# Two layers of a diffusion trunk on one core: the order of transposes, early blocks and residual loads at the seams between stages

## The chip, the cores and the metric

The kernel runs on one core of a Trainium2 chip. The metric is the device time of one execution in microseconds (us); several executions are timed, and the median is given. The engines are called TensorE (PE in the rows), VectorE (DVE), ScalarE (ACT), GpSimd (POOL) and SyncE (SP, which issues most DMAs).

## The reference

Two layers over 1024 latent tokens and 256 context tokens, all of width 1024. The parts that matter here:

```python
for l in range(DEPTH):
    mod = act_lat @ w_mod[l] + b_mod[l]          # shifts, scales and gates of the layer
    sh1, s1, g1, sh2, s2, g2 = [m[:, None, :] for m in jnp.split(mod, 6, axis=-1)]
    ...
    mix = jnp.concatenate([y_pool, y_na, y_gqa], axis=-1) @ w_out[l]
    x = layer_norm(DEEPNORM_ALPHA * x + g1 * mix, ln1_g[l], ln1_b[l])
    ffn = conv_ffn(x * (1 + s2) + sh2, w_up[l], conv_w[l], conv_b[l], w_down[l])
    x = layer_norm(DEEPNORM_ALPHA * x + g2 * ffn, ln2_g[l], ln2_b[l])
```

conv_ffn is an up-projection to 2 x 2816 columns, a convolution of width 3 along the tokens, a * silu(g), and a down-projection. The context tokens go through the same layer with their own modulation, except the last part of layer 1.

## The kernel before, in words

A product in the kernel is exact to float32: each operand is split into a high and a low part (names ending in h and l, `split`: ScalarE makes the high part, VectorE the low one), and three products are added up in PSUM. One such product of 128 x 128 by 128 x 512 is three matmuls. PSUM is used as four tiles of two banks (128 x 1024 f32), handed out in the order of the program and given back when their reader is done.

**Out-projection** (`OutProj`). Eight latent tiles of 128 tokens, then in layer 0 two context tiles. A tile takes 48 matmuls into `oacc`. The first tiles (5 in layer 0, 3 in layer 1) are run with the weight row k outermost, the others one by one. `norm` of a tile: `s` = `oacc` times gate, the input x added, the layer norm (sums on VectorE, Square on ScalarE, the power on GpSimd), `xm` = s * G on GpSimd and + B on VectorE. Its eight transposes (`tps`) are kept in a list `late` and put into PE's order by `follow`, after a tile's products; with `hold` the last call is left out. `NXM` says how many tiles `xm` there are. From tiles 4 to 7, `sums` also forms the sums T1, T2 and T4 of the fast product below and stores them to DRAM (TX2, TX14).

**Up-projection** (`UpLat`) uses a two-by-two scheme of seven products (Strassen's), in 44 half-width blocks. A first part of a block needs only the first four tiles; `early` does it ahead of its place as cover for the last transposes: 24 matmuls into `oe`, ScalarE's copy and VectorE's addition to `ue`. AHEAD is the number of such blocks; all but two are stored to DRAM (UE) and loaded again in `weights`. `end` puts the remaining transposes (T) and early blocks (E) in order by a string of letters. `enter` loads T1, T2 and T4 again, in a pool that opens once the out-projection's has closed.

**Down-projection** (`DownLat`): seven products of 11 units each, a unit being 12 matmuls and a split of loaded pieces (`hw`). A list `later` holds small work to be done at every second unit: loads of the residual tiles `s` from XS, and `residual`, which multiplies them by ln_g and adds ln_b on VectorE.

**Start**: the first shift and scale of all channels (`modps`), as products of 2 x 128 columns; **context FFN's end** (`tail_c`): norm and modulation of the two context tiles for layer 1.

The tile framework sets each engine's order from the program's order, moving work ahead where its operands allow it; `keep_in_program_order` pins an instruction to its place.

## Time and profile before

| | us |
|---|---|
| median of 3 runs | 2997.43 (2996.47 to 3000.92) |
| profiled execution, its own time | 2999.13 |
| span of that execution | 2997.4 |
| TensorE busy | 2784.9 (93%) |
| VectorE busy | 2285.8 (76%) |
| ScalarE busy | 1492.3 (50%) |
| GpSimd busy | 991.3 (33%) |

The span runs from the first to the last instruction; the time has some 1.7 us around it. The busy shares are averages over stages that have different limits, so the rows below go by stretches. The mean granted clock of TensorE over the span is 0.971 of the full 2.4 GHz.

### The profile page before, as it was taken

Reading aid. Unit: us, or ns where it says so; the run is one execution under the profiler, and the core shown is the slowest. Engines: PE = TensorE matmul, PEld = TensorE weight load, DVE = VectorE, ACT = ScalarE, POOL = GpSimd, SP = SyncE. Lnnn points to the kernel's source line nnn. Section 1 sums busy time; section 2 is a strip of 40 time slices with the busy share of each in tenths; the row PEclk is TensorE's granted clock in tenths of the full one; section 3 lists DMA queues with packets and bytes.
Section 4 is the critical chain, followed back from the end, with each engine's and each line's share of the span. In section 5 each row is a group of like instructions: output and inputs, shape, how many; then the busy total and the mean of one; then the engine's idle time right before and its main releaser. Section 6 shows DMA issues by size and latency. Waiting matters only on the chain.

```text
span 2997.4 us, 41914 instructions
## 1 busy us (share of the span) xinstructions
PE 2784.9 (93%) x14715; PEld 2359.7 (79%) x14715; DVE 2285.8 (76%) x3651; ACT 1492.3 (50%) x2328; POOL 991.3 (33%) x773
## 2 busy tenths in 40 slices
PE   8998889988799999899799799999998899999898
PEld 6798778977578887788788679888987688887676
DVE  4985789956688888756887765699957788887667
ACT  4222888824344444434655422598854444444343
POOL 0304354114345554200253440353133444553001
PEclk9999999998899999999899999999999999999999
DMA  7786662164554444865555588452134444445773
GB/s 275 249 269 192 184 169 85 43 219 154 190 168 155 154 152 158 292 211 185 181 177 183 186 269 289 142 171 83 58 121 137 161 158 158 157 159 179 264 222 129
DMA packets 271686, 531.08 MB, mean 177 GB/s; under 512 B 26778, under 2 KB 110834, under 8 KB 270708
## 3 DMA queue, kind: packets, MB, share of 16 engines
q1 hardware_dynamic: 270180, 524.11, 53.9%
q10 hardware_dynamic: 1296, 4.29, 0.4%
q8 instruction: 117, 1.92, 0.3%
q14 instruction: 93, 0.76, 0.1%
HBM read 394.16 MB, written 134.14 MB: 176 GB/s over the span
## 4 chain that ended last, share of the span: by engine, by line
PE 25%; DVE 15%; DMA 10%; issue 4%; ACT 4%; POOL 2%; SPq 1%; POOLq 0%; DVEq 0%; ACTq 0%
PE o L1363 7%; PE dy L1605 4%; PE dx L1605 3%; DVE wl L177 2%; PE pvs L848 2%; PE oacc L1072 2%; PE s L786 2%; DVE wl L172 2%; PE pt L803 1%; DVE s L1329 1%; DMA raw<-in_wup_dram 1%; DMA wm<-in_wmT_dram 1%; DMA VD<-stB 1%; DMA raw<-in_wdown_dram 1%; DVE w L1329 1%
## 5 line engine op out<-in xcount | busy, mean ns | idle before, releaser
L1329 POOL TENSOR_TENSOR cv<-cv 128x512 f32<-128x512 f32 (+1 forms) x110 | 251.5, 2286 | 262.5 <-DVE cv L1499 126.5
L1363 PE MATMUL o<-mxh,wh 128*128 128x512 f32 x640 | 253.5, 397 | 19.3 <-DVE cv L1499 12.7
L177 DVE TENSOR_TENSOR PT<-pt,PT 128x512 fp32r<-128x512 f32 (+2 forms) x396 | 247.8, 644 | 18.4 <-ACT PT L176 16.2
L1363 PE MATMUL o<-mxl,wh 128*128 128x512 f32 x640 | 252.6, 395 | 0.0
L1363 PE MATMUL o<-mxh,wl 128*128 128x512 f32 x640 | 251.6, 394 | 0.0
L786 PE MATMUL s<-K,q 128*128 128x256 f32 (+2 forms) x960 | 236.8, 359 | 14.6 <-DVE m L753 12.8
L176 ACT CAST wh<-raw 128x512 fp32r<-128x512 f32 (+1 forms) x132 | 119.0, 906 | 216.7 <-PE o L1363 141.1
L794 ACT ACTIVATE P<-P,m 128x1280 f32<-128x1280 f32 (+3 forms) x216 | 221.9, 1028 | 9.5 <-DVE m L753 8.0
L177 DVE TENSOR_TENSOR wl<-raw,wh 128x512 fp32r<-128x512 f32 (+1 forms) x132 | 162.8, 1239 | 75.7 <-ACT wh L176 75.1
L176 ACT CAST PT<-pt 128x512 fp32r<-128x512 f32 (+2 forms) x396 | 205.4, 558 | 26.0 <-PE pt L834 10.4
L848 PE MATMUL pvs<-PT,V 128*128 128x256 f32 (+1 forms) x1488 | 209.9, 289 | 5.0 <-DVE PT L177 2.0
L318 PE MATMUL pacc<-wh,mxh 128*128 128x512 f32 (+1 forms) x512 | 191.8, 375 | 15.5 <-DVE rt L284 7.2
L753 DVE CUSTOM_DVE_ANT_0 P<-s,zero,m 128x512 f32<-128x512 f32 (+1 forms) x288 | 189.0, 656 | 20.7 <-PE s L786 1.1
L172 DVE TENSOR_TENSOR wl<-raw,wh 128x1024 fp32r<-128x1024 f32 (+1 forms) x112 | 151.9, 1367 | 62.4 <-ACT wh L170 61.9
L848 PEld LDWEIGHTS pvs<-PT,V 128*128 128x128 f32 x1488 | 186.2, 191 | 12.2 <-ACT mixr L859 4.6
L320 PE MATMUL pacc<-wh,mxl 128*128 128x512 f32 (+1 forms) x512 | 187.5, 367 | 2.2 <-DVE mxl L177 2.2
L319 PE MATMUL pacc<-wl,mxh 128*128 128x512 f32 (+1 forms) x512 | 187.6, 366 | 0.0
L176 ACT CAST wh<-hw 128x1024 fp32r<-128x1024 f32 x98 | 102.7, 1053 | 160.8 <-PE dx L1605 37.5
L177 DVE TENSOR_TENSOR wl<-hw,wh 128x1024 fp32r<-128x1024 f32 x98 | 125.1, 1286 | 75.2 <-ACT wh L176 74.7
L170 ACT CAST wh<-raw 128x1024 fp32r<-128x1024 f32 (+1 forms) x118 | 119.1, 1018 | 93.4 <-POOL raw L168 23.6
L786 PEld LDWEIGHTS s<-K,q 128*128 128x128 f32 x960 | 140.8, 190 | 29.4 <-DVE m L753 23.1
L803 PE MATMUL pt<-ident,P 128*128 128x128 f32 x1032 | 160.1, 273 | 3.5 <-DVE PT L177 2.5
(355 smaller groups left out, 7849.1 us busy)
## 6 DMA issues: line engine op xcount, KB each, us to landing
raw<-in_wup_dram SPq DMA_DIRECT2D x140, 512.0 KB, 4.7
wm<-in_wmT_dram SPq DMA_DIRECT2D x96, 512.0 KB, 4.9
w<-in_wdown_dram SPq DMA_DIRECT2D x44, 512.0 KB, 3.7
hw<-in_wdown_dram SPq DMA_DIRECT2D x66, 256.0 KB, 3.7
q<-QN SPq DMA_DIRECT2D x96, 128.0 KB, 3.1
q<-QG SPq DMA_DIRECT2D x96, 128.0 KB, 2.7
TD0T<-w SPq DMA_DIRECT2D x44, 256.0 KB, 2.2
hw<-HD0S SPq DMA_DIRECT2D x44, 256.0 KB, 3.2
```

The lines of the kernel that those rows point to most:

```text
L172: (sub or nc.vector).tensor_tensor(out=lo[:, :n], in0=raw[:, :n], in1=h[:, :n], op=ALU.subtract)
L176: nc.scalar.copy(h, src)
L177: nc.vector.tensor_tensor(out=lo, in0=src, in1=h, op=ALU.subtract)
L318: nc.tensor.matmul(acc[:, :n], lhsT=xh[:, i, k, :], rhs=wh[:, o:o + n], start=(k == 0), stop=False)
L753: nc.vector.tensor_tensor_reduce(out=dst, in0=src, in1=bias, scale=-1.0, scalar=init, op0=ALU.add, op1=ALU.min, accum_out=m)
L786: nc.tensor.matmul(s[:, :n], lhsT=q[:, part, c0:c0 + P], rhs=K[:, k0:k0 + n], start=(part == 0), stop=(part == 1))
L794: nc.scalar.activation(out=self.P, in_=self.P, func=AF.Exp, bias=self.m, scale=-1.0, accum_out=self.rsum())
L803: nc.tensor.transpose(pt[:, b, :], self.P[:, p0 + b * P:p0 + (b + 1) * P], ident)
L848: nc.tensor.matmul(self.pv[:, c0:c0 + n], lhsT=V[:, vb, :], rhs=x[:, sl, c0:c0 + n], start=(self.c == 0), stop=(self.c == self.tot - 1),)
L1329: eng.tensor_tensor(out=out, in0=a_, in1=b_, op=op)
L1363: nc.tensor.matmul(o, lhsT=lhsT, rhs=rhs, start=fresh and k == 0 and i == 0, stop=k == 3 and i == 2, skip_group_check=not fresh,)
L1605: nc.tensor.matmul(o, lhsT=x[:, tc_], rhs=w[:, r], start=fresh and j == 0 and i == 0, stop=j == NP - 1 and i == 2, skip_group_check=not fresh,
```

## The change

Transposes of the out-projection are taken from `late` by age (AGE = 3 steps, two steps a tile, one after four weight rows, one after eight) instead of by number; layer 0 has three tiles `xm` instead of two; the last latent tile and the context tiles are multiplied on VectorE while ScalarE squares (`gain`: (s + nm) * G with nm the negative mean; `offset`: times the norm's scale, plus B) instead of on GpSimd after the norm. There are 5 and 6 early blocks instead of 4 and 4, kept in halves of 512 columns, the first stored from ScalarE's queue, and all but the last stored and loaded again. T1 and T2 are loaded during the cover, at the letter X, and only T4 in `enter`. In the down-projection the rows g, ln_g, ln_b and the residual tiles are fetched one at a time between units of products 1 and 3, and `residual` is done in products 2 and 4 and pinned. `modps` takes 64 products of 256 columns with 8 loads of 1 MB instead of 128 and 16. The context FFN's end uses `gain` and `offset` too, and the stores to YN go from SyncE instead of ScalarE.

```diff
-NXM = (2, 3)
+NXM = (3, 3)
...
-AHEAD = (4, 4)
+AHEAD = (5, 6)
+AGE = 3
+DORD = ("PE",)
+UEB = (3, 4)
...
-YQ = 1
+YQ = 0
...
+        if early:
+            early(nm)
...
+            if z.lat and t < 7:
+                ln_add(s, xt, op, xt)
+                f = modulate_T(s, G, B, op, "xm", NXM[self.l], self.ps, *dst, ident, False, mul=nc.gpsimd, sink=sink)
+            else:
+                xm = op.tile([P, D], F32, tag="xm", name="xm", bufs=NXM[self.l])
+                nm, rs = ln_add(s, xt, op, xt, False, lambda nm: gain(xm, s, nm, G))
+                offset(xm, xm, rs, B)
+                nb = op.tile([P, 1], F32, tag="lnb", name="lnb", bufs=LNB)
+                nc.vector.tensor_tensor(out=nb, in0=nm, in1=rs, op=ALU.mult)
+                nc.scalar.activation(out=s, in_=s, func=AF.Identity, bias=nb, scale=rs)
+                f = lambda: transpose_T(xm, self.ps, *dst, ident, False, sink)
+            self.late.append((self.step, f))
             if SILU and not self.silu:
                 self.silu = True
                 one = op.tile([P, 1], F32, name="one")
                 nc.scalar.activation(out=one, in_=s[:, 0:1], func=AF.Silu)
-            sink = (lambda pt: self.sums(mx, t - 4, pt)) if z.lat and t >= 4 else None
-            self.late.append(
-                modulate_T(
-                    s, G, B, op, "xm", NXM[self.l], self.ps, mx[0][:, t], mx[1][:, t], ident, False, mul=nc.gpsimd,
-                    sink=sink,
-                )
-            )
...
-        def follow(self, keep=1):
-            while len(self.late) > (keep if len(self.norms) < 2 else 0):
-                self.late.pop(0)()
+        def follow(self):
+
+            self.step += 1
+            if self.late and self.step - self.late[0][0] >= AGE:
+                self.late.pop(0)[1]()
             while self.norms and len(self.late) < NXM[self.l]:
                 self.norm(*self.norms.pop(0))
 
-        def run(self, z, tiles, mx, xin, x1_dst, kmajor=False, hold=False):
+        def run(self, z, tiles, mx, xin, x1_dst, kmajor=False):
             accs = {}
 
             def acc(t):
@@ -1135,31 +1149,33 @@
             if kmajor:
                 for t in tiles:
                     acc(t)
-                for k in range(7):
+                for k in range(8):
                     for t in tiles:
                         self.product(mx, accs[t], t, k)
                     if self.side:
                         self.side()
+                self.norms += [(z, mx, t, accs[t], xin, x1_dst) for t in tiles]
+                self.follow()
+                return
             for t in tiles:
-                if kmajor:
-                    self.product(mx, accs[t], t, 7)
+                acc(t)
+                for k in range(8):
+                    self.product(mx, accs[t], t, k)
+                    if k == 3:
+                        self.follow()
+                self.norms.append((z, mx, t, accs[t], xin, x1_dst))
+                self.follow()
...
+                elif x == "X":
+                    self.take()
...
+        def take(self, proj, xs):
+
+            self.xs = proj.xs = xs
+            for t in proj.stored:
+                y = rawp.tile([P, 1024], F32, tag="raw", name="xt")
+                nc.sync.dma_start(out=y, in_=TX12[t])
+                for i in range(2):
+                    split(xs[i][0][:, t], xs[i][1][:, t], y[:, 512 * i:512 * i + 512].rearrange("p (k j) -> p k j", k=4))
...
-            u = self.uf.tile([P, 1024], F32, tag="ue", name="ue", bufs=2)
-            nc.scalar.copy(u[:, 0:512], o[:, 0:512])
+            u = self.half()
+            nc.scalar.copy(u, o[:, 0:512])
+            if i:
+                nc.scalar.dma_start(out=UE[self.l, f][0], in_=u)
             self.mm(o[:, 512:1024], a_, 512, "B21", True)
-            tt(nc.vector, u[:, 512:1024], o[:, 512:1024], u[:, 0:512], ALU.add)
-            self.blocks[f] = {"early": u, "u1": u[:, 0:512]}
-            if i >= 2:
-                nc.sync.dma_start(out=UE[self.l, f], in_=u)
-                self.blocks[f] = {"early": None}
+            c = self.half()
+            tt(nc.vector, c, o[:, 512:1024], u, ALU.add)
+            if i:
+                nc.sync.dma_start(out=UE[self.l, f][1], in_=c)
+            self.blocks[f] = {"early": None} if i else {"early": c, "u1": u}
+
+        def half(self):
+            return self.uf.tile([P, 512], F32, tag="ue", name="ue", bufs=UEB[self.l])
 
         def cover(self):
             n = AHEAD[self.l]
-            return [lambda i=i: self.early(i) for i in [*range(2, n), 0, 1]]
+            return [lambda i=i: self.early(i) for i in [*range(1, n), 0]]
...
-                if j % 2 and self.later:
+                if (j % 2 or j and p in (1, 3)) and self.later:
...
-            self.later = [lambda t=t: nc.sync.dma_start(out=s[t], in_=x1[t * P:(t + 1) * P, :]) for t in range(4)]
+            pin = tc.keep_in_program_order
+
+            def fetch(t):
+                return lambda: pin(nc.sync.dma_start(out=s[t], in_=x1[t * P:(t + 1) * P, :]))
             self.product(0, X, True, after=lambda t: nc.scalar.copy(u[t], X[t]))
-            self.later = [lambda t=t: residual(s[t]) for t in range(4)]
+            rows = {}
+            self.later = [
+                lambda: rows.update(ln=self.rows()), lambda: rows.update(g2=self.g2())
+            ] + [fetch(t) for t in range(4)]
             Y = self.banks("dy")
             self.product(1, Y, True, after=lambda t, Y=Y: tt(nc.vector, u[t], Y[t], u[t], ALU.add))
...
-            self.later = [lambda t=t: nc.sync.dma_start(out=s[t], in_=x1[t * P:(t + 1) * P, :]) for t in range(4, 8)]
+            self.later += [lambda t=t: residual(rows["ln"], s[t]) for t in range(4)]
             self.product(2, X, False, after=c11)
-            self.later = [lambda t=t: residual(s[t]) for t in range(4, 8)]
+            self.later += [fetch(t) for t in range(4, 8)]
...
+            self.later += [lambda t=t: residual(rows["ln"], s[t]) for t in range(4, 8)]
             self.product(4, X, True, after=c22)
...
-        tt(nc.vector, x, x, rows[0], ALU.mult)
-        tt(nc.vector, x, x, rows[1], ALU.add)
+        for r, op in zip(rows, (ALU.mult, ALU.add)):
+            tc.keep_in_program_order(nc.vector.tensor_tensor(out=x, in0=x, in1=r, op=op))
...
-                for i, t in enumerate(wms):
-                    nc.sync.dma_start(out=t[:, k, :], in_=a["wm0"][8 * (1 - i) + k])
+                t = wms[k // 4][:, k % 4, :]
+                nc.sync.dma_start(out=t, in_=a["wm0"][k])
                 if k % 4 == 0:
                     craw = pp.tile([P, 4, CTX], F32, tag="st", name="craw", bufs=NST)
                     nc.sync.dma_start(out=craw, in_=a["ctxT"][k:k + 4].rearrange("k p t -> p k t"))
                 raw = craw[:, k % 4, :]
                 mp = ps.tile([P, 1024], F32, tag="mm", name="modps")
-                for i, t in enumerate(wms):
-                    for kk in range(8):
-                        nc.tensor.matmul(
-                            mp[0:2, P * i:P * (i + 1)], lhsT=act[:, kk, :], rhs=t[:, k, kk * P:(kk + 1) * P],
-                            start=(kk == 0), stop=(kk == 7),
-                        )
+                for kk in range(8):
+                    nc.tensor.matmul(
+                        mp[0:2, 0:2 * P], lhsT=act[:, kk, :], rhs=t[:, 2 * P * kk:2 * P * (kk + 1)],
+                        start=(kk == 0), stop=(kk == 7),
+                    )
...
-                proj.run(CTXS, range(2), mxc, xin(a["ctx"][0]), XSC, hold=True)
+                proj.run(CTXS, range(2), mxc, xin(a["ctx"][0]), XSC)
                 wxs.close()
                 xss, xsp = right_pool("xs", 1)
-                proj.xs = quarters(xsp)
-                proj.end(up.cover(), "TETEETE")
+                proj.take = lambda: up.take(proj, quarters(xsp))
+                proj.end(up.cover(), "ETEXTEEE")
...
+                xm = fc.tile([P, D], F32, tag="xm", name="xm", bufs=2)
+                junk = fc.tile([P, D], BF16, tag="junk", name="junk")
+                nm, rs = ln_add(s, o, fc, junk, False, lambda nm: gain(xm, s, nm, GB["c"][0]))
+                offset(xm, xm, rs, GB["c"][1])
+                late.append(lambda: transpose_T(xm, ps, xtc[0][:, t], xtc[1][:, t], ident, False))
...
-                proj.end(up.cover(), "ETEETE")
+                proj.end(up.cover(), "EXTEETEEE")
...
+                if not last:
+                    last.extend(row_tile(fd, t_, a[nm][1]) for nm, t_ in (("ln2_g", "l2g"), ("ln2_b", "l2b")))
```

**PE's order at layer 0's passage.** `oacc` are the out-projection's products, `tps` the transposes, `oe` the early blocks, `o` the first block in its place. Before:

```order
L1072 MATMUL oacc<-wh,mxl 128x512 x2
L252 MATMUL tps<-ident,xm 128x128 x16
L1072 MATMUL oacc<-wh,mxh 128x512 x2
...
L252 MATMUL tps<-ident,xm 128x128 x8
L1363 MATMUL oe<-mxh,wh 128x512
...
L1363 MATMUL oe<-mxl,wh 128x512
L1363 MATMUL oe<-mxh,wl 128x512
L1363 MATMUL o_8846<-T2h,wh 128x512
L1363 MATMUL o_8911<-T2h,wh 128x512
L1363 MATMUL o_8846<-T2l,wh 128x512
```

After:

```order
L1078 MATMUL oacc<-wh,mxl 128x512 x2
L258 MATMUL tps<-ident,xm 128x128 x16
L1078 MATMUL oacc<-wh,mxh 128x512 x2
...
L258 MATMUL tps<-ident,xm 128x128 x8
L1377 MATMUL oe<-mxh,wh 128x512
...
L1377 MATMUL oe<-mxl,wh 128x512
L1377 MATMUL oe<-mxh,wl 128x512
L1377 MATMUL o_8823<-T2h,wh 128x512
L1377 MATMUL o_8823<-T2l,wh 128x512
L1377 MATMUL o_8823<-T2h,wl 128x512
```

The first rows are the end of the products with k outermost: 240 ahead of the first transposes before, 288 now. The second piece holds the last transposes, with 24 products of early blocks between them and the first T2 before and 60 now.

**SyncE's order at layer 0's down-projection.** `hw` are weight pieces, g, ln_g, ln_b and s the rows and residual tiles of 512 KB. Before:

```order
L1586 DMA hw<-HD0S_155 128x512
L224 DMA g_11864<-rows0lat_2627 128x1024
L224 DMA ln_g<-in_ln_g_dram 128x1024
L224 DMA ln_b<-in_ln_b_dram 128x1024
L1645 DMA s_11880<-XS_99 128x1024
L1645 DMA s_11881<-XS_99 128x1024
L1645 DMA s_11882<-XS_99 128x1024
L1645 DMA s_11883<-XS_99 128x1024
L1592 DMA hw<-TD0T_166 128x512
L1586 DMA hw<-HD0S_155 128x512
L1592 DMA hw<-TD0T_166 128x512
```

After:

```order
L1601 DMA hw<-HD0S_155 128x512
L228 DMA ln_g<-in_ln_g_dram 128x1024
L228 DMA ln_b<-in_ln_b_dram 128x1024
L1607 DMA hw<-TD0T_166 128x512
L228 DMA g_12108<-rows0lat_2555 128x1024
L1601 DMA hw<-HD0S_155 128x512
L1607 DMA hw<-TD0T_166 128x512
L1663 DMA s_11832<-XS_99 128x1024
L1601 DMA hw<-HD0S_155 128x512
L1607 DMA hw<-TD0T_166 128x512
L1663 DMA s_11833<-XS_99 128x1024
```

Seven loads stood in a row; now ln_g and ln_b are a pair, and each of the others has pieces of a unit around it. The tiles s of the second half follow in product 3.

**VectorE's order at layer 1's down-projection.** `wl` and `mxl` are the splits that products wait for; rows with ln_g and ln_b are the residual. Before:

```order
L177 TENSOR_TENSOR wl<-hw,wh 128x1024 x3
L1329 TENSOR_TENSOR s_26172<-s_26172,ln_g 128x1024
L1329 TENSOR_TENSOR s_26172<-s_26172,ln_b 128x1024
L1329 TENSOR_TENSOR s_26173<-s_26173,ln_g 128x1024
L1329 TENSOR_TENSOR s_26174<-s_26174,ln_g 128x1024
L1329 TENSOR_TENSOR s_26173<-s_26173,ln_b 128x1024
L1329 TENSOR_TENSOR s_26175<-s_26175,ln_g 128x1024
L1329 TENSOR_TENSOR s_26174<-s_26174,ln_b 128x1024
L177 TENSOR_TENSOR mxl<-hw,mxh 128x1024
L1329 TENSOR_TENSOR s_26175<-s_26175,ln_b 128x1024
```

After:

```order
L181 TENSOR_TENSOR wl<-hw,wh 128x1024
L1343 TENSOR_TENSOR u_26148<-dy_26362,u_26148 128x512
L1760 TENSOR_TENSOR s_26154<-s_26154,ln_b 128x1024
L181 TENSOR_TENSOR mxl<-hw,mxh 128x1024
L1760 TENSOR_TENSOR s_26155<-s_26155,ln_g 128x1024
L181 TENSOR_TENSOR mxl<-hw,mxh 128x1024 x2
L1760 TENSOR_TENSOR s_26156<-s_26156,ln_g 128x1024
L1343 TENSOR_TENSOR u_26147<-dy_26361,u_26147 128x512
L1760 TENSOR_TENSOR s_26155<-s_26155,ln_b 128x1024
L1343 TENSOR_TENSOR u_26149<-dy_26362,u_26149 128x512
L181 TENSOR_TENSOR mxl<-hw,mxh 128x1024
```

Before, seven residual operations stand in a row; now they alternate with splits and with the evictions of product 1 (`u`).

## Rows read from the trace of the kernel before

**Rows 1.** Table by stretches (us), core 0; busy time of each engine, TensorE's granted clock

```profile
core 0: us, PE busy (x) PEld busy (x) DVE busy (x) ACT busy (x) POOL busy (x), PEclk, DMA share, GB/s
12.00:39.00 27.00, 27.00 (x245) 20.24 (x243) 11.59 (x37) 6.67 (x12) 0.00 (x0) 1.00 0.96 366
665.00:751.00 86.00, 66.74 (x300) 54.79 (x299) 54.48 (x90) 42.46 (x52) 38.01 (x23) 0.88 0.48 164
751.00:866.00 115.00, 89.00 (x350) 70.27 (x349) 86.60 (x88) 48.28 (x64) 40.73 (x23) 0.87 0.52 178
866.00:1000.00 134.00, 133.69 (x590) 110.21 (x589) 111.03 (x104) 60.49 (x71) 64.74 (x34) 1.00 0.44 148
1250.00:1300.00 50.00, 40.93 (x163) 32.11 (x162) 37.34 (x34) 19.26 (x22) 0.00 (x0) 0.90 0.76 266
2188.00:2283.00 95.00, 92.49 (x425) 76.76 (x424) 44.45 (x64) 39.39 (x47) 35.21 (x29) 0.98 0.40 132
2283.00:2480.00 197.00, 176.01 (x734) 140.74 (x733) 160.78 (x159) 86.12 (x111) 88.96 (x47) 0.95 0.48 159
2777.00:2820.00 43.00, 29.42 (x108) 22.32 (x109) 30.06 (x26) 14.55 (x16) 0.00 (x0) 0.84 0.78 280
```

**Rows 2.** TensorE's waits by releaser, 665 to 866: us in total, times, longest

```profile
PE tps L252 <- DVE xm L263: 19.3, 5, 13.3
PE o L1363 <- ACT T2h L176: 8.8, 1, 8.8
PE oe L1363 <- ACT ue L1422: 5.5, 2, 4.7
PE tps L252 <- DVE lnm L235: 3.7, 1, 3.7
PE o L1363 <- DVE cv L1499: 3.3, 1, 3.3
PE o L1363 <- ACT u L1443: 3.3, 1, 3.3
PE o L1363 <- DVE T2l L177: 1.5, 1, 1.5
```

**Rows 3.** The same view, 2188 to 2480 us (layer 1's passage)

```profile
PE tps L252 <- DVE xm L263: 9.0, 3, 3.6
PE o L1363 <- ACT T2h L176: 6.0, 1, 6.0
PE o L1363 <- DVE cv L1499: 4.2, 2, 3.5
PE oe L1363 <- ACT ue L1422: 2.1, 2, 1.4
PE o L1363 <- ACT u L1443: 1.8, 1, 1.8
...
```

**Rows 4.** TensorE's timeline: start, us, engine, line, operation, tiles, count, idle before

```profile
699.53 1.06 PE L252 MATMUL tps<-ident,xm 128*128 128x128 f32 x8 [1.20 <-DVE xm L263]
```

**Rows 5.** TensorE's waits by releaser, 1250 to 1300 us (down, layer 0)

```profile
PE dy L1605 <- ACT wh L176: 4.9, 1, 4.9
PE dy L1605 <- DVE wl L177: 4.0, 2, 2.6
```

**Rows 6.** The same view, 2777 to 2820 us (down, layer 1)

```profile
PE dy L1605 <- ACT mxh L176: 8.5, 1, 8.5
PE dy L1605 <- DVE mxl L177: 4.5, 2, 2.6
...
```

**Rows 7.** VectorE's timeline at the start of layer 0's down-projection

```profile
...
1252.82 1.23 DVE L1329 TENSOR_TENSOR s<-s,ln_g 128x1024 f32<-128x1024 f32 x1 [5.24 <-DMA s<-XS]
```

**Rows 8.** Timeline at the end of the context FFN, three engines

```profile
1693.25 2.37 ACT L246 ACTIVATE acc<-acc,lnb,lrs 128x1024 f32<-128x1024 f32 x2
...
1696.80 2.35 DVE L263 TENSOR_TENSOR xm<-xm,ln_b 128x1024 f32<-128x1024 f32 x2
...
1698.16 2.15 PE L252 MATMUL tps<-ident,xm 128*128 128x128 f32 x9 [7.57 <-DVE xm L263]
```

128 lines of the change are left out of this document (53 added, 75 removed).

## The prediction

> **What bounds the kernel now.** I read the page first: TensorE is busy 93% of the span, so the kernel is bound by it wherever nothing interrupts it, and the only time to win lies where it waits or runs slowly. The table by stretches shows where that is [rows 1]. From 866 to 1000 us, inside an up-projection, TensorE is busy 133.69 of 134.00 us at a granted clock of 1.00; its 590 products of 512 columns there cost 133.69 / 590 = 0.2266 us each, my price for one at the full clock, 2.4 GHz. Three kinds of stretch look otherwise: the passage from the out-projection to the up-projection in layer 0 (665 to 866 us) and in layer 1 (2188 to 2480), and the start of each down-projection (1250 to 1300 and 2777 to 2820). There TensorE idles, and the clock column falls to 0.84 to 0.95.
>
> What each costs, from [rows 1] and one price more, 1.06 us for the eight transposes of a tile [rows 4]:
> Layer 0 passage: busy 66.74 + 89.00 = 155.7 of 201 us, idle 45.3. Its 650 records are 80 transposes (ten tiles) and 570 products; at the full clock 570 x 0.2266 + 10 x 1.06 = 139.8, so 15.9 us more went to the half clock (1.2 GHz).
> Layer 1, 2283 to 2480: busy 176.0 of 197; 694 products and some 40 transposes are 162.6, so 13.4 us of half clock and 21 idle.
> Down, layer 0: 40.9 of 50 busy, 163 x 0.2266 = 36.9: 4.0 of clock, 9.1 idle. Down, layer 1: 29.4 of 43, 108 x 0.2266 = 24.5: 4.9 of clock, 13.6 idle.
> Together about 125 us: the most that this change could return there.
>
> The waits by releaser name the idle time. In layer 0 [rows 2]: transposes waiting for the normalised tile (xm, 19.3 us, the longest 13.3), T2h 8.8 and T2l 1.5, an early block's eviction (ue) 5.5, lnm 3.7, then 6.6 for u and cv. In layer 1 the same with smaller sizes [rows 3]: xm 9.0, T2h 6.0, cv 4.2, ue 2.1, u 1.8. At the down-projections the weight pieces are late: wh and wl 8.9 us [rows 5], mxh and mxl 13.0 [rows 6]. Why they are late shows on VectorE: it idles 5.24 us for a residual tile (s<-XS) and then works through residual operations that stand in its queue ahead of the splits the products need [rows 7].
>
> **The change part by part.**
> **Transposes by age, layer 0.** The long wait of 13.3 us is for the first normalised tile, whose time is set by the loads and the chain of the norm, not by TensorE; the change doesn't hasten it. It puts a sixth tile's products into it: 48 x 0.2266 = 10.9 us. Were nothing else in the way, 2.4 us of wait would be left. But all four PSUM tiles are then held by products, and the first transposes need a slot that the eviction of the third tile frees, which itself waits for a buffer s; I take 5 us left, so 8.3 saved. The other 6.0 us of xm waits may return between later tiles, since the norm of a pair of tiles is as long as before; I take none saved. Bounds 0 and 14.
> **S-sums loaded during the cover.** T2h and T2l, 10.3 us, are late because their reloads start only when the out-projection's pool has closed: in PE's order before, 24 early products (5.4 us) lie between the last transposes and the first use of T2. Now the reloads are issued ahead of the last transposes, and 60 products (13.6 us) follow those. I take 10 saved; bounds 6 and 10.3.
> **Fifth early block.** 24 products more (5.4 us) are moved into the passage from the stage behind it, so PE's sum doesn't change; as cover they take from ue 5.5 and lnm 3.7 what isn't VectorE's. The last tiles' multiply leaves GpSimd as well. I take 4 of 9.2; bounds 0 and 9.
> Of the 15.9 us of clock, which goes with the waits, I take 6, near their share (22 of 45 us saved would be 8). Layer 0: -8.3 - 10 - 4 - 6 = **-28**, bounds -10 and -50.
> **Layer 1.** T2h -6; of xm's 9.0 us -4 (the transposes are already spread there, the change shifts them by half a tile); ue and u -1; clock -5 of 13.4. **-16**, bounds -6 and -32.
> **Down-projections.** Before, SyncE issues g, ln_g, ln_b and four s tiles, seven of 512 KB, in a row ahead of the next weight pieces. At 366 GB/s, the rate of a stretch with the DMA engines 0.96 busy [rows 1], these 3.67 MB hold the pieces back by 10 us; the wait was 8.9 and 13.0. Now one such tile goes with each unit, and a unit lasts 12 x 0.2266 = 2.72 us: 0.52 MB of it and 0.52 MB of pieces take 2.87 us, 0.15 over for each of some seven units. That is nearly no slack, but the pieces are fetched ahead. The residual operations now lie in product 2 and product 4, one operation between two splits by pinning: 11 splits and 8 residual operations of 1.23 us [rows 7] and 8 half-wide additions (half of it, an estimate) are 28.3 us in 11 x 2.72 = 29.9 us of products. It fits, barely; were it uncovered, it would cost 3 us a layer. Layer 0: 7 of 9.1 idle and 3 of 4.0 clock, **-10** (bounds -4, -13). Layer 1: 10 of 13.6 and 4 of 4.9, **-14** (bounds -6, -18).
> **Context FFN's end.** TensorE waits 7.57 us for xm, behind a ScalarE pass of 2.37 us and two multiplies of the same length that now run beside the squares [rows 8]. Up to 4.7 leave the chain, but VectorE has to find room for the multiply; **-3**, bounds -1 and -4.7.
> **Start.** TensorE is back to back there: 245 records in 27.00 us are 110 ns each [rows 1], or 0.86 ns a column, twice the 0.443 of the 512-column products. So columns set it, and half as many records save next to nothing; the first transfer is 0.52 MB longer, 1.4 us at 366 GB/s. **+1**, bounds -1 and +2.
> **Queues.** The YN stores go from ScalarE's queue to SyncE's, the first halves of the early blocks the other way; weight loads may now stand behind a store that waits for its data. I take 0, bounds -1 and +3.
> Sum: -28 - 16 - 10 - 14 - 3 + 1 = **-70** on the profiled execution's 2999.13 us: 2929. The median, 2997.43, lies 1.7 below it, so I predict **2928**.
>
> **The rivals.**
> *VectorE takes over.* It was busy 86.6 of 115 us and 160.8 of 197 in the passages, and each wait filled leaves it less time. If only T2, half of the down terms and the context's end return: -10 - 6 - 12 - 3 = -31, with some clock **2964**. Against it: 866 to 1000 runs TensorE without waits with VectorE at 111 of 134, 83%; layer 0's 141 us of work in 173 would be 82%.
> *The waits are cut into small ones and the clock stays low.* The clock terms (6 + 5 + 3 + 4 = 18) don't come: -52, **2947**. The row against it is 2188 to 2283, where transposes and products already alternate on the same four PSUM tiles, at 0.98. The Trainium skill, "TensorE: Matmul & The Clock Gate", section "A second HAM failure mode: psum-queue depth-cycling", says that cycling through PSUM can make TensorE pause between groups so often that the gain is lost to re-throttling. By that rule this rival would be the likeliest; the row just named doesn't bear it out.
> *More than I take.* All xm and ue waits vanish with most of the clock: layer 0 -48, layer 1 -28, down -30, the rest -3: -109, **2890**. For it, nothing in TensorE's own work stands against it (its products at the full clock leave 125 us unused); against it, the first tile's norm, which no early block hastens.
> *Slower.* One mechanism: the early blocks kept in DRAM (four and five) are reloaded in halves into three or four buffers on SyncE's queue. If a reload waits there for its buffer, the block's weight loads wait behind it, and TensorE with them. It cancels the gain at 70 / 9 = 8 us a block; at 9 us, **3009**. For it, weights loaded once a block; against it, two or three blocks of 13 us lie between a buffer's use and its reload.
> *No change to speak of.* The norm's chain keeps its waits and the DMA rate keeps the down waits, and T2's 16 us are given back in queues: within 0.2%, 6 us, which is about what a measurement of this kernel can tell from none: **2997**.
>
> **How the numbers follow.** Forecast (2905 to 2952, with the clock rival at its upper edge) 0.58, of which the clock rival 0.15; VectorE 0.21; more than I take 0.13; slower 0.04; no change 0.04. The range leaves out the last two and the outer third of the VectorE and high cases: 2895 to 2968. Faster by over 0.2%: 0.92; within: 0.04; slower: 0.04.
>
> **What would show it.** After a right step, T2h and T2l are gone from the waits in both layers; the first transposes' wait is about 5 us rather than 13.3; the context products end some 8 us earlier after the out-projection's start; the down starts show no wait over 3 us and a clock above 0.95; TensorE's busy time falls by 10 to 20 us though its products are the same (half clock gone). It is wrong if new waits stand at the early blocks' reloads (ue<-UE ahead of raw), if VectorE passes 90% in a passage while TensorE waits for a split, or if the waits for xm are the same sum in more pieces.

## The result, and the profile after

The changed kernel takes 2972.60 us (median of 3, 2970.17 to 2972.66) where the kernel before takes 2997.43: a ratio of 0.9902, 95% interval 0.9884 to 0.9919. It is faster by 1%, some 25 us, and not by the 70 of the forecast; 2972.6 lies above the range. The profiled execution has a span of 2970.8 us (before 2997.4).

TensorE's timeline cuts the span into stages: each begins with the first product of its kind (`oacc`, `o`, `dx`, the second `pacc`), so a stage's length is the difference of two start times. The last stage ends with TensorE's last product, 12 us before the span does in both.

| stage | before | after | difference | predicted |
|---|---|---|---|---|
| start and attention, layer 0 | 610.6 | 615.0 | +4.4 | +1 |
| layer 0, out-projection and cover | 188.0 | 180.7 | -7.3 | -28 with the next line |
| layer 0, up-projection | 410.7 | 406.4 | -4.3 | |
| layer 0, down-projection and its end | 466.4 | 459.0 | -7.4 | -10 |
| context end, attention, layer 1 | 512.7 | 512.8 | +0.1 | -3 |
| layer 1, out-projection and cover | 139.4 | 133.8 | -5.6 | -16 with the next line |
| layer 1, up-projection | 412.3 | 417.9 | +5.6 | |
| layer 1, down-projection | 245.2 | 233.0 | -12.2 | -14 |

The table by stretches of the kernel before, for the two covers and the two up-projections at these limits (columns as in [rows 1]):

```profile
610.57:798.57 188.00, 150.71 (x660) 122.63 (x657) 120.52 (x167) 69.13 (x89) 65.62 (x47) 0.90 0.61 211
798.57:1209.31 410.74, 399.33 (x1718) 325.83 (x1718) 335.25 (x316) 179.85 (x211) 191.64 (x99) 0.98 0.46 155
...
2188.46:2327.88 139.42, 122.35 (x547) 100.15 (x544) 82.22 (x106) 58.99 (x77) 54.78 (x39) 0.96 0.45 151
2327.88:2740.19 412.31, 401.23 (x1716) 324.83 (x1717) 340.42 (x321) 180.95 (x213) 196.78 (x102) 0.99 0.47 157
```

And of the changed kernel:

```profile
614.96:795.63 180.67, 155.14 (x672) 125.92 (x669) 118.29 (x170) 69.31 (x90) 51.35 (x40) 0.91 0.66 227
795.63:1202.05 406.42, 395.58 (x1706) 321.59 (x1706) 337.86 (x317) 180.04 (x211) 195.38 (x103) 0.99 0.48 162
...
2173.88:2307.73 133.85, 127.82 (x584) 105.30 (x581) 85.78 (x113) 62.92 (x83) 50.14 (x38) 0.96 0.50 175
2307.73:2725.65 417.92, 397.88 (x1681) 320.13 (x1680) 339.20 (x318) 179.32 (x211) 199.09 (x102) 0.98 0.48 160
```

Read layer 1's two lines together. By the program the cover now holds two early blocks more, 48 products or 10.9 us, and it is still 5.6 us shorter: like for like it won 16.5, the forecast's 16. The up-projection behind it has these 48 products less and is 5.6 us longer: in this pair of profiles it lost the same 16.5. TensorE's idle time falls from 17.1 to 6.0 us in the cover (139.42 - 122.35 and 133.85 - 127.82) and rises from 11.1 to 20.0 in the up-projection. This profile is the longest of four with the same code for layer 1 (below); by their mean some 12 us are lost again, and about 5 remain. So the question of this study is who takes back in the up-projection what the cover wins.

In layer 0, TensorE's waits by releaser from 665 to 866 us (against [rows 2]):

```profile
PE oe L1377 <- ACT wh L180: 8.5, 1, 8.5
PE tps L258 <- DVE xm L269: 5.4, 3, 3.6
PE tps L258 <- DVE s L1088: 4.1, 2, 2.9
...
PE o L1377 <- ACT wh L180: 2.9, 1, 2.9
```

The transposes wait 9.5 us instead of 23.0 (one product of the out-projection 1.5), T2h and T2l are gone, and a new wait of 8.5 us stands at the weights of an early block, which the prediction had taken as 0, at most 3 (its queues). In layer 1, 2188 to 2480 us (against [rows 3]), no wait for xm or T2h is left, and weights are waited for too:

```profile
PE o L1377 <- ACT wh L180: 5.9, 2, 3.8
PE oe L1377 <- ACT wh L180: 5.1, 1, 5.1
PE o L1377 <- DVE cv L1514: 4.0, 2, 2.7
```

The starts of the two down-projections, shifted with their stage (against the fifth and the last row of [rows 1]):

```profile
1243.00:1293.00 50.00, 46.16 (x194) 36.96 (x193) 31.77 (x29) 22.41 (x24) 0.00 (x0) 0.97 0.74 244
2762.00:2805.00 43.00, 41.17 (x176) 32.02 (x175) 22.56 (x20) 20.63 (x23) 0.00 (x0) 1.00 0.84 293
```

There the change does what was said: 194 products instead of 163 in 50 us of layer 0, 176 instead of 108 in 43 us of layer 1.

### The profile page after: what moved, and what is told of

The parts are those of the page before. It is cut to its first block, busy times and chain, and to the rows that moved or that the text cites. A ratio compares the mean times of both kernels' runs of the same rounds, so it can differ in the third digit from the quotient of the medians.

```text
span 2970.8 us, 41688 instructions
## 1 busy us (share of the span) xinstructions
PE 2782.5 (94%) x14587; PEld 2344.0 (79%) x14587; DVE 2293.0 (77%) x3656; ACT 1493.1 (50%) x2329; POOL 980.7 (33%) x769
## 5 line engine op out<-in xcount | busy, mean ns | idle before, releaser
L181 DVE TENSOR_TENSOR PT<-pt,PT 128x512 fp32r<-128x512 f32 (+2 forms) x396 | 247.8, 645 | 17.7 <-ACT PT L180 15.2
L1377 PE MATMUL o<-mxh,wh 128*128 128x512 f32 x616 | 244.2, 397 | 11.3 <-DVE cv L1514 5.8
L1377 PE MATMUL o<-mxh,wl 128*128 128x512 f32 x616 | 242.9, 395 | 0.9 <-DVE wl L181 0.9
L1377 PE MATMUL o<-mxl,wh 128*128 128x512 f32 x616 | 243.0, 395 | 0.0
```

Source lines behind the costliest of these rows:

```text
L181: nc.vector.tensor_tensor(out=lo, in0=src, in1=h, op=ALU.subtract)
L1377: nc.tensor.matmul(o, lhsT=lhsT, rhs=rhs, start=fresh and k == 0 and i == 0, stop=k == 3 and i == 2, skip_group_check=not fresh,)
```

## The experiments

The same code differs from one profile to the next. Layer 1's two stages take 551.8, 546.6, 546.3 and 540.8 us (mean 546.4) in the four profiles whose code is the same there (after, E1, E1b and E10), and the up-projection alone 409.3 to 417.9. So a difference between two single profiles shows little unless it is clear of that spread. Ratios are to the kernel before on the same chip, with 95% intervals; the kernel before had medians of 2995.7 to 3003.7 there, so times are compared by ratio.

### E4: the down-projection alone

The kernel before with DownLat of after and nothing else:

```diff
-                if j % 2 and self.later:
+                if (j % 2 or j and p in (1, 3)) and self.later:
...
+            self.later += [fetch(t) for t in range(4, 8)]
```

> The kernel before with the down-projection's edit alone (rows and residual tiles fetched between units, residual pinned in products 2 and 4). Theory (this part acts by itself, as the two traces say: 5.6 us in layer 0, 12.1 in layer 1): about 2980 us, 17 to 18 under the kernel before in the same job. Rival (its gain needs the rest of the change, such as the YN stores' queue): under 10.

0.9944 (0.9926 to 0.9961), 2984.65 against 3001.67: -17 us. The down stages are shorter by 6.8 and 8.8. By ratio this edit gives 0.56 of the 0.98 per cent of the whole change, more than half, where 24 us were forecast for it.

### E1, E1b: the first shift and scale

E1 puts the products of 128 columns back; E1b keeps 256 columns and issues the small stores of the context's rows from ScalarE's queue, since SyncE issues one of them ahead of all eight loads of x:

```diff
-                    nc.sync.dma_start(out=AROW[z], in_=r[0:1, :])
+                    nc.scalar.dma_start(out=AROW[z], in_=r[0:1, :])
```

SyncE's timeline after, at 51 us; before, the first `xraw` was issued at 48.34, ahead of that store:

```profile
51.08 0.24 SPq L1840 DMA_DIRECT2D AROWctx<-arctx  x1
51.41 0.34 SPq L1789 DMA_DIRECT2D xraw<-in_xT_dram  x1
```

> The changed kernel with the first shift and scale as before (128 products of 2x128, 16 loads of 512 KB). Theory: the new products moved SyncE's order so that the first load of x stands behind a store (AROWctx) that waits for ScalarE, and the projection starts 4.4 us late; undone, about 2968 us, the out-projection of layer 0 begins at about 610.5 us instead of 615.0, and TensorE's wait for mxh near 65 us is about 1 us again. Rival: the 4.4 us come from elsewhere; 2972.6 and 615.

> The changed kernel, products of 256 columns kept, with only the two AROW stores issued from ScalarE's queue, so that no load of x stands behind one. Theory (the queue's order is the cause, not the products): about 2968 us, out-projection of layer 0 begins at about 610.5 us. Rival (the wide products or their larger loads are the cause): 2972.6, 615.

E1: 0.9915 (0.9898 to 0.9932); E1b: 0.9904 (0.9888 to 0.9919). Neither total differs from the change's; E9 against E8 (below), the same edit as E1, is 0.9861 against 0.9886, with intervals that just overlap. By stages the edit does cost: the out-projection begins at 607.5 to 612.9 us (mean 610.4) in the six profiles with 128 columns, and at 611.7 to 617.9 (mean 614.9) in the fourteen with 256. The price there is +4.5, not +1. In E1b the first x load goes out at 49.46 and TensorE's wait for mxh falls from 3.51 to 2.02 us (1.05 before), but the stage stays at 614.0: SyncE's order is a part of the cause at most, and the rest is open.

### E3, E6: the reloads of T1 and T2 in the cover

SyncE's timeline after, around the new wait of layer 0 (`raw` weights, `TX` the stored sums, `xt` their reload):

```profile
742.14 0.33 SPq L1401 DMA_DIRECT2D raw<-in_wup_dram  x1
742.57 0.98 SPq L1387 DMA_DIRECT2D xt<-TX  x1
...
754.00 0.32 SPq L1387 DMA_DIRECT2D xt<-TX  x1
762.13 0.32 SPq L1129 DMA_DIRECT2D TX<-xq  x1
...
768.34 0.57 SPq L1387 DMA_DIRECT2D xt<-TX  x1
768.96 1.20 SPq L1401 DMA_DIRECT2D raw<-in_wup_dram  x2
```

and TensorE, which waits for the first of these two weights:

```profile
775.97 0.80 PE L1377 MATMUL oe<-mxh,wh 128*128 128x512 f32 x1 [8.47 <-ACT wh L180]
```

For 26.8 us no weights are issued: the reload of the fourth tile stands in the queue ahead of them and waits for that tile's sums, which have first to be formed and stored. E3 puts the letter X (where the reloads are issued) later; E6 also gives the reloads buffers of their own:

```diff
-                proj.end(up.cover(), "ETEXTEEE")
+                proj.end(up.cover(), "ETETEEXE")
...
-                proj.end(up.cover(), "EXTEETEEE")
+                proj.end(up.cover(), "EEXTETEEE")
...
-                y = rawp.tile([P, 1024], F32, tag="raw", name="xt")
+                y = proj.op.tile([P, 1024], F32, tag="s", name="xt", bufs=SBUFS[self.l])
```

> The changed kernel with the reload of T1 and T2 put two early blocks later in layer 0 and one later in layer 1, so that fewer weight loads stand behind reloads that wait for their stores in SyncE's queue. Theory: TensorE's waits for wh of an early block (8.5 us in layer 0, 5.1 in layer 1) go to 2 or less; 2960 to 2968 us, where the up-projection gives part of it back. Rival (the loads are late for their buffers or the transfer rate): the same waits at another place, 2971 to 2974.

> The changed kernel with T1 and T2 reloaded as late as in the run e3 and into the norm's buffers s instead of the three buffers that weight loads rotate through. Theory (queue and buffers both make the early blocks wait): layer 0's passage from the out-projection's first product to the first block falls from 180.7 us to 170 to 174, TensorE's waits for an early block's wh under 2 us in sum; 2958 to 2965 us. Rival (something else is as late, ue or the norm): the passage stays at 179 to 182, 2969 to 2973.

E3: 0.9903 (0.9888 to 0.9918), nothing. The wait for an early block's weights falls from 8.5 to 1.4 us in layer 0, so the place in the queue is its cause; but the transposes wait 16.9 us instead of 9.5, and the cover takes 181.6 us, as before. E6: 0.9884 (0.9869 to 0.9900), 2967.23: by ratio about 5 us, with an interval that overlaps the change's. In E6 layer 0's cover takes 173.4 us instead of 180.7 and no early block waits for weights, as the theory said; but its up-projection takes 411.3 instead of 406.4. TensorE's waits in E6 from 790 to 866 us, behind the cover:

```profile
PE o L1377 <- DVE cv L1514: 5.4, 2, 3.6
PE o L1377 <- ACT T2h L180: 3.9, 1, 3.9
PE o L1377 <- DVE wl L181: 2.4, 2, 1.5
```

So taking 8.5 us of wait away is worth some 5 us by the ratio, which is not clear of noise: the rest returns as waits for transposes, cv and T2h, at other places.

### E2, E7, E8, E9: how many early blocks

```diff
-AHEAD = (5, 6)
+AHEAD = (4, 4)
```

The strings of letters are shortened to match. E7 has (4, 2). E8 is four and four with E6's reloads; E9 is E8 with the first shift and scale of before.

> The changed kernel with 4 early blocks in each layer instead of 5 and 6. Theory: a block whose first part is done early is paced by VectorE and the loads, so the 24 products moved out of it are not saved there; with fewer early blocks the time stays within 4 us of 2972.6, and layer 1's stretch from out-projection to down-projection stays 552 us or falls. Rival (the blocks are needed as cover): each block taken away costs its 5.4 us, 2984 to 2989.

> The changed kernel with 4 early blocks in layer 0 and 2 in layer 1. Theory (an early block saves nothing in its place, and two are enough cover): layer 1 from out-projection to down-projection 527 to 537 us (551.8 with six, 537.0 with four), 2953 to 2962 us. Rival (the cover is needed): TensorE waits for xm and T2 again at the passage, 5 to 12 us, 2967 to 2975.

> Four early blocks in each layer (as in e2) together with the later reload of T1 and T2 into the norm's buffers (as in e6). Theory (two separate causes, the number of blocks and SyncE's queue): layer 1 from out-projection to down-projection 532 to 537 us, layer 0's 582 to 586; 2955 to 2962 us, under every kernel so far. Rival (both take away the same wait): as e2, 2962 and more.

> e8 with the first shift and scale as before too. Theory (its new products cost 3 to 5 us by SyncE's order): the out-projection of layer 0 begins at 607 to 611 us instead of 612 to 617; 2951 to 2958 us. Rival (what is won there is given back behind it, since e1's time did not fall): the time of e8.

E2: 0.9876 (0.9859 to 0.9894); E7: 0.9903 (0.9888 to 0.9919); E8: 0.9886 (0.9870 to 0.9903); E9: 0.9861 (0.9847 to 0.9876), 2958.71 us, the fastest kernel that leaves nothing out (E17, below, equals it). Layer 1's two stages take 537.0 (E2), 538.0 (E8), 538.6 (E9) and 539.4 us (E17) with four blocks, 543.2 with two, and 540.8 to 551.8, in the mean 546.4, with six. In E7 a wait for T2h is back (5.5 us), as its rival had it: two blocks are too little cover in layer 1, and six too many.

In the whole time this is less clear. E2's interval overlaps the change's. E8's theory of two separate causes failed: with four blocks and E6's reloads together it is no faster than E2 or E6 (0.9884) alone, so the gains of the two edits don't add up.

### E5, E11: relief for single engines

E5 puts the two subtractions that form `s` of an early block on GpSimd; E11 reloads `ue` from ScalarE's queue:

```diff
+            eng = nc.gpsimd if "early" in b else nc.vector
-            tt(nc.vector, s[:, lo], rg[:, lo], rg[:, hi], ALU.add)
+            tt(eng, s[:, lo], rg[:, lo], rg[:, hi], ALU.add)
...
-                    nc.sync.dma_start(out=b[n], in_=UE[self.l, f][i])
+                    nc.scalar.dma_start(out=b[n], in_=UE[self.l, f][i])
```

> The changed kernel with the two sums of weights of each block whose first part is done early made on GpSimd instead of VectorE (1.4 us of VectorE less a block, 11 blocks). Theory (VectorE paces those blocks): 2960 to 2967 us, layer 1's blocks from out-projection's end to down-projection 5 us or more shorter. Rival (the loads, in their three buffers and SyncE's queue, pace them, and GpSimd takes twice as long for a sum): 2972 to 2980.

> The changed kernel with the halves of early blocks loaded again from ScalarE's queue instead of SyncE's. Theory (with six blocks the weight loads of layer 1 stand in SyncE's queue behind these loads, which wait for a buffer): TensorE's waits for wh in layer 1's first blocks (3.8 and 2.2 us) fall by half or more; 2962 to 2968 us. Rival (weight loads wait for other things, stores that VectorE makes late and their own buffers): the same waits; 2971 to 2976.

E5: 0.9901 (0.9884 to 0.9918); E11: 0.9905 (0.9888 to 0.9921); layer 1 545.6 and 546.0. Neither helps. E5's theory, that VectorE paces these blocks, forecast 2960 to 2967 us and failed with 2971.87. E11 speaks against the prediction's slower rival: the place of ue's reloads in SyncE's queue isn't what holds these blocks.

### E12 to E14: the down weights' sums at other blocks

`sum_w` loads down weights, forms their sums on VectorE, four operations of 512 columns, and stores them, after the up blocks numbered in SUMS. E12 begins with them behind the six early blocks, E13 puts them close together at the start, E14 is E9 with the first behind its four blocks:

```diff
-SUMS = [2, 4, 6, 8, 10, 12, 14, 16, 18, 19, 20]
+SUMS = [7, 8, 10, 11, 12, 13, 14, 16, 18, 19, 20]
```

> The changed kernel with the sums of the down-projection's weights (sum_w: two loads, four sums on VectorE, four stores) moved out of the first six blocks of each up-projection (from blocks 2 and 4 to 7 and 11). Theory (in blocks whose first part is done early SyncE's queue is the pace: weight loads stand behind these sums' stores, and two of three load buffers are theirs): layer 1 from out-projection to down-projection 536 to 541 us instead of 546, layer 0's 3 to 5 us shorter; 2961 to 2967 us. Rival (VectorE and ScalarE's chain of a block is the pace): both as before, 2970 to 2975.

> The opposite dose: five of these sums in the first six blocks instead of two. Theory (queue): each costs 3 to 5 us there and is not won back later, layer 1 556 us or more; 2985 to 2995 us. Rival (chain of a block): under 3 us in each layer, 2972 to 2978.

> e9 (four blocks, later reload into the norm's buffers, first shift and scale as before) with the sums moved out of the first five blocks. Theory (queue): 3 to 6 us from the two layers together, 2952 to 2956 us. Rival: as e9, 2958 to 2960.

E12: 0.9936 (0.9921 to 0.9951); E13: 0.9946 (0.9928 to 0.9964); E14: 0.9901 (0.9884 to 0.9918). All are worse than the versions they start from. But look at E12's layer 1 by stretches, ahead of it that of the changed kernel, both from the up-projection's start:

```profile
2307.00:2389.00 82.00, 71.56 (x294) 56.60 (x294) 62.95 (x63) 35.10 (x44) 33.02 (x18) 0.96 0.52 168
2389.00:2449.00 60.00, 54.50 (x216) 42.38 (x215) 49.87 (x44) 23.96 (x28) 27.82 (x16) 0.92 0.49 169
2449.00:2549.00 100.00, 99.73 (x434) 81.20 (x433) 81.31 (x77) 44.24 (x51) 48.18 (x25) 1.00 0.42 140
2549.00:2726.00 177.00, 173.18 (x747) 140.82 (x747) 146.14 (x138) 76.64 (x90) 90.06 (x44) 0.99 0.49 166
```

E12:

```profile
2318.00:2400.00 82.00, 75.25 (x323) 60.16 (x324) 60.89 (x64) 39.42 (x49) 35.88 (x22) 1.00 0.44 148
2400.00:2460.00 60.00, 60.00 (x264) 49.23 (x263) 48.00 (x43) 26.63 (x30) 29.59 (x17) 1.00 0.40 139
2460.00:2560.00 100.00, 94.40 (x406) 75.33 (x405) 85.11 (x80) 42.16 (x51) 46.19 (x25) 1.00 0.49 169
2560.00:2730.00 170.00, 163.78 (x702) 132.25 (x701) 141.07 (x134) 72.36 (x84) 82.10 (x42) 0.99 0.52 175
```

Without sums in the first 142 us TensorE gets 587 products done instead of 510, 77 x 0.2266 = 17.4 us more, and the clock is full. (The three other profiles of the changed kernel's code there have 531, 537 and 552, so the difference is some 8 to 17 us.) Behind them the sums stand closer together, and it falls back: 1108 products in 270 us, 4.10 a us, where the changed kernel does 4.26. Layer 1's two stages as a whole take 545.2 us with none of the sums in the first six blocks (E12), 546.4 with two and 546.8 with five (E13). The queue theory's 536 to 541 and 556 or more both failed. The place of these sums, loads and stores together decides where TensorE waits; moving them only moves the wait.

### E15, E16: the sums left out, six and four early blocks

Both leave out the four subtractions of every `sum_w`, in both layers; loads and stores stay, so products T1 to T4 of the down-projection work with other weights than the reference's. E15 is the changed kernel, E16 is E2.

```diff
-        tt(nc.vector, w0[:, lo], w0[:, hi], w0[:, lo], ALU.subtract)
-        tt(nc.vector, w0[:, hi], w1[:, hi], w0[:, hi], ALU.subtract)
-        tt(nc.vector, w1[:, hi], w1[:, hi], w0[:, lo], ALU.subtract)
-        tt(nc.vector, w1[:, lo], w1[:, lo], w1[:, hi], ALU.subtract)
```

> The changed kernel without the four VectorE subtractions of each sum_w (44 in a layer, 512 columns each; the loads and stores of the weights stay, so the down-projection works with wrong weights in products T1 to T4). In the trace of the changed kernel these operations take 1.4 us each beside GpSimd, so 45.9 us for 32 of them in 2400 to 2700 us. Theory V: the blocks behind an early part have 60 products instead of 84 (13.6 us instead of 19.0) and nearly the same VectorE work, so with six of them in a row TensorE waits for VectorE, and what the cover gained is lost there. Then layer 1's passage with its up-projection falls from about 546 us to 537 or less, the difference to four blocks (the next run) is 2 us or less, and the whole time is some 2952. Rival Q: the blocks are held by SyncE's queue and the buffers, the loads come as late as before, layer 1 stays within 3 us of 546 and the difference to four blocks stays about 8 us; the whole time is 2965 to 2972.

> Four early blocks in each layer, without the subtractions of sum_w as in the run before it (the same part left out). Theory V: less to gain here, since four short blocks hold VectorE up less: layer 1 from 537 to some 533, whole time about 2952, equal to that of six blocks within 0.1%. Rival Q: as four blocks with the sums, layer 1 537, whole time 2958 to 2962, 8 to 10 us ahead of six blocks without sums.

Layer 1's up-projection of E15 by stretches, from its start:

```profile
2305.24:2387.24 82.00, 74.14 (x310) 59.72 (x309) 59.93 (x60) 37.34 (x46) 34.93 (x20) 0.96 0.60 194
2387.24:2447.24 60.00, 59.84 (x262) 48.79 (x261) 45.60 (x43) 28.09 (x33) 31.58 (x19) 1.00 0.48 170
2447.24:2706.93 259.69, 259.69 (x1136) 213.19 (x1135) 193.05 (x175) 119.22 (x136) 105.78 (x65) 1.00 0.48 162
```

From the 82nd us on TensorE has practically no idle time left. Layer 1's two stages take 533.0 us with six blocks (546.4 in the mean with the sums) and 530.7 with four (537.0): six blocks gain 13 us by it, four gain 6, and the difference between them goes from 9 to 2.3. So these sums are what most of the idle time in layer 1's up-projection hangs on, and Q's number there (within 3 us of 546) failed.

Which way they act isn't shown. The stores stay, but they no longer wait for VectorE. SyncE's waits in the first 142 us of layer 1's up-projection, in the changed kernel and then in E15:

```profile
SPq L1583 <- DVE w L1343: 27.8, 10, 6.8
...
SPq L1579 <- DMA w<-in_wdown_dram: 23.5, 8, 3.4
```

In the changed kernel weight loads stand behind such stores. One case, SyncE first, then VectorE, which waits for these weights, and TensorE, which waits for their split, its longest wait in these 142 us:

```profile
2358.95 0.68 SPq L1583 DMA_DIRECT2D TD1T<-w  x1
2359.69 0.71 SPq L1401 DMA_DIRECT2D raw<-in_wup_dram  x1
...
2365.78 0.69 DVE L1343 TENSOR_TENSOR s<-s,raw 128x512 f32<-128x512 f32 x1 [0.71 <-DMA raw<-in_wup_dram]
...
2369.65 0.50 PE L1377 MATMUL o<-T2h,wh 128*128 128x512 f32 x1 [3.75 <-ACT wh L180]
```

So the sums can cost TensorE time by VectorE's own order (theory V), or by stores that wait for VectorE and hold the weight loads behind them. E15 and E16 take both away at once, E12 moves both, and no run separates them.

In the whole time the difference between six and four blocks didn't shrink: 0.26% with the sums (0.9902 and 0.9876), 0.27% without (E15 0.9827, 0.9805 to 0.9849; E16 0.9800, 0.9784 to 0.9817), intervals that overlap each time; the sums cost either kernel the same, 0.75 and 0.76%. V's forecast of equal totals failed, and the 7.4 us between the medians are near Q's 8 to 10. In the two profiles 9.3 us lie between the spans, of which layer 1's stages hold 2.3 and the last down-projection 5.0 (235.4 and 230.4); that isn't explained, and is of the size of the spread between profiles.

### E17: the sums on GpSimd

```diff
-        tt(nc.vector, w0[:, lo], w0[:, hi], w0[:, lo], ALU.subtract)
+        tt(nc.gpsimd, w0[:, lo], w0[:, hi], w0[:, lo], ALU.subtract)
```

and the other three likewise, in E9.

> The fastest version so far (four blocks, reloads of T1 and T2 late and in buffers of their own, first shift and scale in products of 128 columns as before) with the subtractions of sum_w on GpSimd instead of VectorE; nothing is left out. GpSimd is busy 64 of 130 us in a steady stretch of the up-projection and a half-wide subtraction of it takes 1.3 to 1.8 us, so its share would go to some 0.65. Theory V: VectorE gets some 45 us of time back in each up-projection, TensorE's waits for cv and o shrink, and the time falls from 2958.7 to some 2950. Rival P: VectorE's operations get longer whenever GpSimd works beside them (512 columns 0.69 us alone, up to 2.3 beside it), so what leaves VectorE comes back in its other operations, and the time stays at 2958 or rises by up to 10 us.

0.9862 (0.9845 to 0.9879), the same as E9. VectorE's groups of 2400 to 2700 us in E9 (shapes, count, busy us, mean ns):

```profile
L181 DVE TENSOR_TENSOR wl<-raw,wh 128x1024 fp32r<-128x1024 f32 x31 | 47.7, 1537 | 27.3 <-ACT wh L180 27.2
...
L1343 DVE TENSOR_TENSOR o<-o,u 128x512 f32<-128x512 f32 x47 | 32.2, 689 | 1.0 <-PE o L1377 1.0
L1343 DVE TENSOR_TENSOR w<-w,w 128x512 f32<-128x512 f32 x18 | 26.3, 1460 | 0.0
L1343 DVE TENSOR_TENSOR w<-w 128x512 f32<-128x512 f32 x17 | 25.2, 1480 | 3.4 <-DMA w<-in_wdown_dram 3.1
...
L1343 DVE TENSOR_TENSOR s<-raw 128x512 f32<-128x512 f32 x15 | 13.1, 875 | 0.1
```

and in E17:

```profile
L181 DVE TENSOR_TENSOR wl<-raw,wh 128x1024 fp32r<-128x1024 f32 x31 | 55.2, 1787 | 10.0 <-ACT wh L180 9.5
...
L1343 DVE TENSOR_TENSOR o<-o,u 128x512 f32<-128x512 f32 x47 | 32.5, 692 | 23.1 <-PE o L1377 17.0 <-ACT u L1481 4.0 <-issue 2.1
L1343 DVE TENSOR_TENSOR s<-raw 128x512 f32<-128x512 f32 x15 | 27.9, 1858 | 0.7
```

The sums' 51.5 us have left VectorE, but its busy time falls by only 7.7 (247.8 to 240.1): `s<-raw` goes from 875 to 1858 ns, `wl<-raw` from 1537 to 1787. Rival P is right.

### E10: the context's end

While the context ends, eight latent tiles (`xin`) are multiplied by ln_g and get ln_b added for layer 1's residual, on GpSimd. E10 does the first three on VectorE:

```diff
+                eng = nc.vector if t < 3 else nc.gpsimd
-                nc.gpsimd.tensor_tensor(out=x, in0=x, in1=prev[0], op=ALU.mult)
+                eng.tensor_tensor(out=x, in0=x, in1=prev[0], op=ALU.mult)
```

In the changed kernel the transposes there wait 4.9 us instead of 7.6 in the kernel before, but the next wait grows from 4.9 to 8.1, for `rt`, whose scale `rrs` waits on GpSimd behind three of those tiles:

```profile
1686.52 7.09 POOL L2002 TENSOR_TENSOR xin<-xin,ln_g 128x1024 f32<-128x1024 f32 x3 [6.55 <-DMA ln_g<-in_ln_g_dram]
1693.56 0.88 POOL L287 TENSOR_TENSOR rrs<-ss,neghalf 128x2 f32<-128x2 f32 x1
```

> The changed kernel with the residual rows of the first three tiles of layer 1 (two passes a tile) made on VectorE instead of GpSimd. Theory (after the context FFN's end TensorE no longer waits for the transposes but for rt, behind 7 us of these passes in GpSimd's queue): TensorE's wait of 8.1 us for rt falls under 4; 2966 to 2970 us. Rival (rt waits for a load or for VectorE): the same wait, 2972 and more.

The wait for rt falls to 3.9 us, but the stage takes 522.7 us, the longest of all profiles (512.8 to 520.4 in the other kernels with the change's code there), and the time is 2975.66, 0.9916 (0.9902 to 0.9931), not better than the change. What takes the gain back isn't shown.

## Why the prediction was wrong, point by point

The sum was 43 us too large: 16 in each layer's passage, 4 in the down-projections, 3 each at the context's end and the start. (Its last step gives 2927 rather than 2928, which changes nothing.)

**Layer 1's passage (-16): the failing step.** The waits named in [rows 3] went (no wait for xm or T2h is left), and TensorE's idle time in the cover fell by 11.1 us, the 11 that were forecast in waits. The step that failed is the assumption that products moved into the cover leave the stage behind them as it was, "so PE's sum doesn't change", as it says of the fifth block. That stage's idle time rose by 8.9 us (11.1 to 20.0), and TensorE's busy time in the two stages rose by 2.1 instead of falling by 5 of clock.

The VectorE rival was dismissed by the stretch from 866 to 1000, with 83% of VectorE, but that stretch holds whole blocks of 84 products. A block whose early part is done has 60 left, 13.6 us, and nearly the same VectorE work. [rows 1] had it: 111.03 of 134 us is 15.8 us of VectorE for the 19.0 us of a whole block; less the one split that is done early, 1.23 us in E12's timeline, 14.6 remain for 13.6 of TensorE. This is an estimate. It gives a reason for the sign and not the size (1 us a block, where six blocks lose some 4 a block against four), and VectorE isn't full there: 62.95 + 49.87 of the first 142 us (79%), so the prediction's own sign for this, over 90%, didn't show. What the runs do show is narrower: with the weights' sums gone, layer 1's two stages are 13 us shorter with six blocks and 6 with four. Whether the sums cost it by VectorE's order or by the stores that wait for them stays open, and so does the reason why six blocks lose more than four.

**Layer 0's passage (-28).** The waits went nearly as worked out (transposes 23.0 to 9.5 us, the first of them 13.3 to 2.9 where 5 was taken; T2 gone). What was missing are two other terms: 8.5 us of new wait at an early block's weights (the next point), and the clock's 6, since TensorE's busy time in the two stages is 550.7 us where it was 550.0. The up-projection, with 5.4 us of products less, got 4.3 shorter. When E6 takes the new wait away, the cover is 7.3 us shorter and the up-projection 4.9 longer, so there too most of it is given back; no run without sums resolves layer 0, since E15 and E16 differ by 1.4 us.

**Queues (0).** Mis-sized: 8.5 us in layer 0's cover, where reloads that wait for their own store stand ahead of weights (E3), and 5.1 in layer 1's, which go only when the reloads have buffers of their own too (E6). The prediction had priced stores that wait for data at up to 3. Some 5 us of the 13.6 are real time by E6's ratio, with overlapping intervals.

**Fifth and sixth block.** The prediction counted on 4 us for the fifth block in layer 0 and on 1 us of ue and u in layer 1, where two were added; four and four (E2) is faster by ratio, 0.9876 against 0.9902, though these intervals overlap. E9's and the change's don't, but E9 differs in two more edits.

**Down-projections (-24).** Right mechanism, size a little off. At the start of the stages 31 and 68 more products get done in the same time, 7.0 and 15.4 us at 0.2266, where the sum had 10 and 14; over the whole stages 7.4 and 12.2 are left, and E4 alone measures 17.

**Context's end (-3).** Came 2.7 in its own wait and was given back in the next, by a queue on GpSimd that the prediction didn't look at.

**Start (+1).** Mis-sized, +4.5 by the mean of twenty profiles. The columns do set the products' time, as argued: sixteen records of 256 columns take 3.62 us, sixteen of 128 take 1.91. The later loads of x are a part of the price; the rest is open.

**The clock.** The 11 us of clock counted in the passages didn't come: the granted clock is 0.91 in layer 0's cover (0.90 before) and 0.96 in layer 1's (0.96). There the rival "the clock stays low" was right, and TensorE's busy time fell by 2.4 us, not by 10 to 20. In the down starts the clock rose from 0.90 and 0.84 to 0.97 and 1.00, as counted. It goes with the waits: E12's first 142 us of layer 1's up-projection run at 1.00 where the changed kernel, with more idle time on the same four PSUM tiles, has 0.96 and 0.92. The rule of the Trainium skill, "TensorE: Matmul & The Clock Gate", section "A second HAM failure mode: psum-queue depth-cycling", that TensorE's short pauses while PSUM banks are cycled make the clock swing, is not needed for that, and no run here tells it apart.

The result lies between two rivals, VectorE (2964) and no change (2997). That it is nearer the first is no proof of it: that rival counted only half of the down terms and nothing of the transposes' waits, and here most of both came. The runs bear out a part of it, VectorE's sums, at a place that the prediction didn't cost.

## What to carry to other kernels

Work that is moved forward as cover for the bound engine leaves behind it a stage with the same work for all the others: before pulling a block's products ahead, divide the other engines' time per block by what is left of it, not by the whole block (here this gives the sign; the cause isn't shown). More cover is not always better: in layer 1's two stages four blocks beat two and six. In SyncE's queue a store or reload that waited for its data held the loads behind it (26.8 us at 742 us); look for such waits in the queue's own view, and give a reload buffers of its own (the later place alone gained nothing here). A gain at a stage's start is to be read off at the stage's end, and a single profile is not enough for it.
